# RWKV-7 decay: the low-rank product per pair in channel-major form, and the running sum by a scan

## The chip, the cores and the metric

The kernel runs on one core of a Trainium2 chip. The metric is the device time of one execution in microseconds (us), median of several runs. TensorE is PE in the profile (PEld its weight loads), VectorE is DVE, ScalarE is ACT, GpSimd is POOL and SyncE is SP. A line such as L621 is a line of the kernel before, unless it is said to be of the changed one.

## The reference

One decoder block over 512 tokens of width 2048: an input projection, RWKV-7 time mixing (16 heads of 64) beside sliding-window attention, gated merge, output projection, and a gated convolutional FFN. The change touches only the decay of the time mixing:

```python
w = -jax.nn.softplus(-(w0 + jnp.tanh(wd) @ w2)) - 0.5
decay = jnp.exp(-jnp.exp(w.astype(f32)))
...
def step(state, inp):
    r_t, k_t, v_t, w_t, ka_t, kb_t = inp
    sa = jnp.einsum('bhvk,bhk->bhv', state, ka_t)
    state = (state * w_t[:, :, None, :] + sa[..., None] * kb_t[:, :, None, :]
             + v_t[..., None] * k_t[:, :, None, :])
    y = jnp.einsum('bhvk,bhk->bhv', state, r_t)
    return state, y
```

Here wd has 96 columns and w2 is 96 x 1024. The recurrence over 512 steps is computed in chunks of 64 steps, for which the kernel needs, per channel, the product of the decays from the start of a chunk up to each step. Since exp(w) = exp(-0.5) * sigmoid(w0 + tanh(wd) @ w2), the logarithm of that product is a running sum of sigmoids times -exp(-0.5).

## The kernel before

The weights of the big projections are f32 values split into two f32r parts (whi, wlo), and so are the activations (xhi, xlo); a 128x128 block of weights takes three products (L260 to L262, output acc, 512 tokens wide). ScalarE makes whi, VectorE makes wlo. DMAs fill four raw tiles ahead of that.

After the first norm comes attention, then the RWKV stage, about 315 to 1205 us of the span. It works on eight pairs of heads (128 channels each). Each pair p goes through three functions:

- early(p) projects k, r and v, and makes the normalised keys and the decays. Here is the change. thw (tanh(wd), with a row of ones for w0) is computed once, 128 x 512 with the low rank on partitions.
- late(p) builds the chunk matrices, inverts triangular systems in five rounds of f16 products (L728 to L751), and walks the eight chunks (L755 to L772): psG (two halves of 64 rows), copy G on VectorE, psU, two copies UV (ScalarE the upper half, VectorE the lower), psS (two halves), update SV on VectorE, and from there the next psG. L779 and L781 beside them collect the output.
- final(p) normalises and gates the output.

The calls stand in the order late(p), early(p+1), final(p), and then three gate projections. The order in which each engine issues is not the order of the code: a scheduler in the tile framework builds it from dependencies and its own estimates, and it interleaves the projection products and early(p+1) with the chunk walk of late(p), so that TensorE has other work while VectorE and ScalarE pass results along the chain. Each engine then issues its list strictly in that order, waiting on semaphores.

In early(p) the decay goes like this before the change. Four products of 128 tokens (L621) take thw as the stationary operand and w2 as the moving one, so that tokens lie on partitions: ps[tokens, channels]. ScalarE applies Tanh, VectorE adds 1 (L624; with 0.5 * (tanh(x/2) + 1) this is twice the sigmoid). Four more products (L628) with the constant K["tri"], ones where two tokens are in the same chunk and in order, sum over tokens and turn the result around: ps[channels, tokens]. Two Exp (L629, L631) make Et, the decay product with a leading column of ones, and Ei, its inverse. Et and Ei are used in late(p), in BKK and BAR (L666 to L669), which feed the first products L689. bulk is a ring of three PSUM tiles, shared by nearly all products of the stage.

Of the kernel before, what the change touches and what calls it, by code (L numbers as in the profile page):

```python
# [8 lines left out]
F32 = mybir.dt.float32  # L9
# [3 lines left out]
AF = mybir.ActivationFunctionType  # L13
ALU = mybir.AluOpType
# [4 lines left out]
P = 128  # L19
S = 512  # L20
NT = S // P
HD = 64
C = 64
# [5 lines left out]
SQE = float(np.exp(-0.5))  # L29
# [5 lines left out]
class Dims:  # L35
# [37 lines left out]
CONST_PARTS = (  # L73
    ("ident", 128), ("strict", 64), ("incl", 64), ("istack", 64),
    ("m1", 64), ("m2", 64), ("m4", 64), ("m8", 64), ("m16", 64), ("m32", 64),
    ("t1bd", 128), ("idsg", 128), ("tri", 128), ("bo", 128), ("cen", 128), ("sel2", 2), ("ones", 128), ("dist", 256),
)
CONST_AT = {}
_at = 0
# [6 lines left out]
def shape_constants():  # L86
    out = np.zeros((P, NCONST), np.float32)

    def put(nm, a):
        o, n = CONST_AT[nm]  # L90
        out[:, o : o + n] = a
# [4 lines left out]
    t = np.arange(C)[None, :]  # L96
# [7 lines left out]
    si, ti = i[:, None], i[None, :]  # L104
    put("t1bd", (si == ti) | ((si // 2 == ti // 2) & (si > ti)))
    same = si // C == ti // C
    put("tri", same & (si <= ti))
    put("bo", same)
    put("cen", (si == ti) - same / float(C))
    put("sel2", si // C == np.arange(2)[None, :])  # L110
# [2 lines left out]
    dist = (BLK + si - kj).astype(np.float32)  # L113
# [21 lines left out]
def block_kernel(ctx: ExitStack, tc: tile.TileContext, d: Dims, a: dict, out: bass.AP):  # L135
    nc = tc.nc
    act, dve, pool, pe, sync = nc.scalar, nc.vector, nc.gpsimd, nc.tensor, nc.sync
# [145 lines left out]
    if True:  # L283
# [233 lines left out]
        with ExitStack() as pr:  # L517
# [21 lines left out]
            def bulk():  # L539
                return blk.tile([P, S], F32, name="bulk", tag="bulk")  # L540
# [15 lines left out]
            for i in range(NG):  # L556
                acc = ztile(d.c_gd + i * P)
                t = wtile("lw")
# [19 lines left out]
            pool.memset(SV[C:P, 0, 1], 0.0)  # L578
            Et = bd.tile([P, NCH, C + 1], F32, name="Et")
            pool.memset(Et[:, :, 0:1], 1.0)  # L580
            AI = bd.tile([P, 2, NCH, P], F16, name="AI")
            BT = bd.tile([P, 2, NCH, P], F16, name="BT")
            def r3(ap, c=C):
                return ap.rearrange("p (n c) -> p n c", c=c)
# [14 lines left out]
            def early(p):  # L599
# [16 lines left out]


                ps = bulk()
                for t in range(NT):
                    ts = slice(t * P, (t + 1) * P)  # L620
                    pe.matmul(ps[:, ts], thw[:, ts], w2, start=True, stop=True)  # L621
                lg = wtile("lw")
                act.activation(lg, ps, AF.Tanh, scale=0.5)
                dve.tensor_scalar(lg, lg, 1.0, None, op0=ALU.add)  # L624
                ps = bulk()
                for t in range(NT):
                    ts = slice(t * P, (t + 1) * P)
                    pe.matmul(ps[:, ts], lg[:, ts], K["tri"], start=True, stop=True)  # L628
                act.activation(Et[:, :, 1:], r3(ps), AF.Exp, scale=-0.5 * SQE)  # L629
                Ei = wtile("Ei")  # L630
                act.activation(Ei, ps, AF.Exp, scale=0.5 * SQE)  # L631

                ps = bulk()
                lora(ps, ag, 0, 1)
# [772 lines left out]
```

## Time and profile before

| what | value |
|---|---|
| time, median of 3 runs | 2952.3 us (2951.39 to 2952.68) |
| span of the profiled execution (first to last instruction) | 2946.4 us |
| TensorE busy | 2897.7 us, 98% |
| VectorE busy | 1949.0 us, 66% |
| ScalarE busy | 1316.0 us, 45% |
| GpSimd busy | 219.4 us, 7% |
| mean granted TensorE clock | 0.997 |
| chain that ended last, by engine | PE 92%, DVE 3%, ACT 2%, DMA 2% |

The page gives the span of the profiled execution and no other time of it; the median of the runs stands 5.9 us above that span. Busy time of TensorE is modelled from overlapping matmuls, so its share says that the queue is never empty for long, not that each product runs at its best; the distance from one start to the next tells what a product costs.

### The profile page before, as it was taken

Reading aid. Unit: us, or ns where it says so; the run is one execution under the profiler, and the core shown is the slowest. Engines: PE = TensorE matmul, PEld = TensorE weight load, DVE = VectorE, ACT = ScalarE, POOL = GpSimd, SP = SyncE. Lnnn points to the kernel's source line nnn. Section 1 sums busy time; section 2 is a strip of 40 time slices with the busy share of each in tenths; the row PEclk is TensorE's granted clock in tenths of the full one; section 3 lists DMA queues with packets and bytes.
Section 4 is the critical chain, followed back from the end, with each engine's and each line's share of the span. In section 5 each row is a group of like instructions: output and inputs, shape, how many; then the busy total and the mean of one; then the engine's idle time right before and its main releaser. Section 6 shows DMA issues by size and latency. Waiting matters only on the chain.

```text
span 2946.4 us, 48467 instructions
## 1 busy us (share of the span) xinstructions
PE 2897.7 (98%) x18922; PEld 2473.2 (84%) x18922; DVE 1949.0 (66%) x3242; ACT 1316.0 (45%) x2134; POOL 219.4 (7%) x286
## 2 busy tenths in 40 slices
PE   7999999999999999999999899999999999999999
PEld 6777777777777777688888899999999999888887
DVE  5555666666666666344567877778777778665555
ACT  4344434434334334232346554554554555544444
POOL 0001000000000000101000011011011011000000
PEclk9999999999999999999999999999999999999999
DMA  6855656656656656878877788888888888877775
GB/s 185 210 151 153 178 139 154 159 129 161 158 131 162 155 129 170 250 223 262 275 243 247 193 242 236 230 227 225 234 239 235 227 229 237 311 240 242 256 258 189
DMA packets 225142, 609.47 MB, mean 207 GB/s; under 512 B 24768, under 2 KB 44944, under 8 KB 223888
## 3 DMA queue, kind: packets, MB, share of 16 engines
q1 hardware_dynamic: 157504, 434.92, 45.9%
q0 software_dynamic: 36064, 132.14, 23.3%
q10 hardware_dynamic: 31344, 39.31, 3.9%
q8 instruction: 148, 2.42, 0.3%
q14 instruction: 82, 0.67, 0.1%
HBM read 556.62 MB, written 174.43 MB: 248 GB/s over the span
## 4 chain that ended last, share of the span: by engine, by line
PE 92%; DVE 3%; ACT 2%; DMA 2%; issue 1%; ACTq 0%; SPq 0%; DVEq 0%
PE X L1108 17%; PE X L975 11%; PE acc L262 10%; PE acc L261 10%; PE acc L260 10%; PE Y L975 8%; PE Y L1108 8%; PE Z L1108 4%; PE psG L758 1%; PE bulk L689 1%; PE mi L505 1%; PE bulk L751 1%; PE psS L769 1%; PE bulk L728 1%; DMA raw<-in_w_z_dram 1%
## 5 line engine op out<-in xcount | busy, mean ns | idle before, releaser
L262 PE MATMUL acc<-xhi,wlo 128*128 128x512 f32 x1120 | 460.0, 411 | 0.7 <-DVE wlo L244 0.7
L260 PE MATMUL acc<-xhi,whi 128*128 128x512 f32 x1120 | 454.9, 406 | 4.0 <-ACT whi L243 4.0
L261 PE MATMUL acc<-xlo,whi 128*128 128x512 f32 x1120 | 453.9, 405 | 0.0
L243 ACT ACTIVATE whi<-raw 128x512 fp32r<-128x512 f32 x352 | 220.0, 629 | 491.3 <-PE acc L261 326.2
L968 DVE TENSOR_TENSOR wlo<-raw,whi 128x1024 fp32r<-128x1024 f32 x210 | 257.0, 1224 | 203.4 <-ACT whi L967 202.4
L244 DVE TENSOR_TENSOR wlo<-raw,whi 128x512 fp32r<-128x512 f32 x352 | 240.3, 688 | 205.1 <-ACT whi L243 198.1
L967 ACT ACTIVATE whi<-raw 128x1024 fp32r<-128x1024 f32 x210 | 222.6, 1060 | 289.3 <-PE X L975 151.8
L1108 PE MATMUL X<-b,whi 128*128 128x256 f32 x1472 | 270.4, 284 | 2.3 <-DVE u L1128 0.9
L1108 PE MATMUL X<-t,whi 128*128 128x256 f32 x1408 | 258.9, 284 | 8.7 <-DVE u L1128 8.3
L1091 DVE TENSOR_TENSOR wlo<-raw,whi 128x1024 fp32r<-128x1024 f32 x176 | 215.1, 1223 | 77.5 <-ACT whi L1090 77.2
L1108 PE MATMUL Y<-t,whi 128*128 128x256 f32 x1408 | 257.1, 283 | 0.0
L262 PEld LDWEIGHTS acc<-xhi,wlo 128*128 128x128 f32 x1120 | 211.3, 189 | 44.2 <-issue 3.1
L260 PEld LDWEIGHTS acc<-xhi,whi 128*128 128x128 f32 x1120 | 211.6, 189 | 43.2 <-ACT whi L243 5.2
L261 PEld LDWEIGHTS acc<-xlo,whi 128*128 128x128 f32 x1120 | 211.3, 189 | 40.3 <-issue 3.1
L1090 ACT ACTIVATE whi<-a 128x1024 fp32r<-128x1024 f32 x132 | 139.3, 1056 | 216.4 <-DVE a L1084 213.2
L1108 PEld LDWEIGHTS X<-b,whi 128*128 128x128 f32 x1472 | 230.7, 193 | 3.1 <-issue 2.4
L1108 PEld LDWEIGHTS X<-t,whi 128*128 128x128 f32 x1408 | 220.8, 193 | 9.3 <-DVE u L1128 5.7
L1108 PEld LDWEIGHTS Y<-t,whi 128*128 128x128 f32 x1408 | 219.6, 192 | 0.0
L1108 PE MATMUL X<-b,wlo 128*128 128x256 f32 x736 | 209.1, 284 | 2.1 <-DVE wlo L1091 2.1
L1091 DVE TENSOR_TENSOR wlo<-a,whi 128x1024 fp32r<-128x1024 f32 x132 | 161.7, 1226 | 68.2 <-ACT whi L1090 67.6
L1108 PE MATMUL X<-t,wlo 128*128 128x256 f32 x704 | 200.1, 284 | 0.1
L1108 PE MATMUL Y<-t,wlo 128*128 128x256 f32 x704 | 199.2, 283 | 0.0
(346 smaller groups left out, 6151.2 us busy)
## 6 DMA issues: line engine op xcount, KB each, us to landing
raw<-in_w_up_dram SPq DMA_DIRECT2D x180, 512.0 KB
raw<-in_w_z_dram SPq DMA_DIRECT2D x288, 256.0 KB
s_dn<-in_w_dn_dram POOLq DMA_DIRECT2D x88, 512.0 KB, 6.3
raw<-in_w_up_dram POOLq DMA_DIRECT2D x88, 512.0 KB, 8.7
raw<-s_dn SPq DMA_DIRECT2D x88, 512.0 KB
raw<-in_w_dn_dram SPq DMA_DIRECT2D x66, 512.0 KB
a<-in_w_up_dram SPq DMA_DIRECT2D x48, 512.0 KB
s_dn<-in_w_dn_dram SPq DMA_DIRECT2D x44, 512.0 KB
```

Source lines behind the costliest of these rows:

```text
L243: pin(act.activation(hi, raw, AF.Copy))
L244: pin(dve.tensor_tensor(lo, raw, hi.bitcast(F32), op=ALU.subtract))
L260: pe.matmul(acc, whi[:, j], xhi[:, k], start=first, stop=False)
L261: pe.matmul(acc, whi[:, j], xlo[:, k], start=False, stop=False)
L262: pe.matmul(acc, wlo[:, j], xhi[:, k], start=False, stop=last)
L505: pe.matmul(ps[:, h], pT[:, kb, h], vt[:, n - 1 + kb, g * HD : (g + 1) * HD], start=kb == kbs[0], stop=kb == kbs[-1])
L967: act.activation(whi, wr, AF.Copy)
L968: dve.tensor_tensor(wlo, wr, whi.bitcast(F32), op=ALU.subtract)
L975: pe.matmul(dst, l[:, q, ts], r[:, es], start=fst and j == 0, stop=lst and j == 2, skip_group_check=True)
L1090: pin(act.activation(hi, t, AF.Copy))
L1091: pin(dve.tensor_tensor(lo, t, hi.bitcast(F32), op=ALU.subtract))
L1108: pin(pe.matmul(ps, l[:, k], r[:, k], start=start and k + i == 0, stop=last and i == 2, skip_group_check=True))
```

## The change

The product is formed channel-major at once: w2 is the stationary operand and thw, all 512 tokens of it, the moving one, so that one product gives ps[channels, tokens]. Tanh and the +1 are the same instructions on that layout. The running sum is then one instruction on VectorE, tensor_tensor_scan along the 512 tokens: state = going * state + lg, where the tile going holds ones, and a zero at the first token of each chunk, so that the sum starts anew there. It writes Ei; the first Exp reads Ei and writes Et, and the second turns Ei into its inverse in place. The constant "tri" leaves the table of constants (128 columns less), and GpSimd fills going once, before the pairs.

```diff
-    ("t1bd", 128), ("idsg", 128), ("tri", 128), ("bo", 128), ("cen", 128), ("sel2", 2), ("ones", 128), ("dist", 256),
+    ("t1bd", 128), ("idsg", 128), ("bo", 128), ("cen", 128), ("sel2", 2), ("ones", 128), ("dist", 256),
...
-    put("tri", same & (si <= ti))
...
+            going = bd.tile([P, S], F32, name="going")
+            pool.memset(going, 1.0)
+            pool.memset(going.rearrange("p (n c) -> p n c", c=C)[:, :, 0:1], 0.0)
...
                 ps = bulk()
-                for t in range(NT):
-                    ts = slice(t * P, (t + 1) * P)
-                    pe.matmul(ps[:, ts], thw[:, ts], w2, start=True, stop=True)
+                pe.matmul(ps, w2, thw, start=True, stop=True)
                 lg = wtile("lw")
                 act.activation(lg, ps, AF.Tanh, scale=0.5)
                 dve.tensor_scalar(lg, lg, 1.0, None, op0=ALU.add)
-                ps = bulk()
-                for t in range(NT):
-                    ts = slice(t * P, (t + 1) * P)
-                    pe.matmul(ps[:, ts], lg[:, ts], K["tri"], start=True, stop=True)
-                act.activation(Et[:, :, 1:], r3(ps), AF.Exp, scale=-0.5 * SQE)
                 Ei = wtile("Ei")
-                act.activation(Ei, ps, AF.Exp, scale=0.5 * SQE)
+                dve.tensor_tensor_scan(Ei, going, lg, 0.0, op0=ALU.mult, op1=ALU.add)
+                act.activation(Et[:, :, 1:], r3(Ei), AF.Exp, scale=-0.5 * SQE)
+                act.activation(Ei, Ei, AF.Exp, scale=0.5 * SQE)
```

The scheduler makes new lists from this, in the RWKV stage alone. On TensorE, before, in early(2) beside the chunk walk of pair 1, this stood from the first triangle product (L628: bulk<-cst,lw) to the psU that follows the product for the learning rate (L597):

```order
L628 MATMUL bulk<-cst,lw 128x128
L769 MATMUL psS<-UV,KK 64x64
L779 MATMUL bulk<-MM,UV 64x64
L781 MATMUL bulk<-BAR,SV 64x64
L628 MATMUL bulk<-cst,lw 128x128 x2
L758 MATMUL psG<-SV,AB 64x64
L628 MATMUL bulk<-cst,lw 128x128
L758 MATMUL psG<-SV,AB 64x64
L597 MATMUL bulk<-ads,wl 128x512
L762 MATMUL psU<-G,BX 128x64
```

Just ahead of that stand the four L621 (bulk<-wl,thw), cut up in the same way by a psG, and then an acc, the psU and two acc of that chunk. In the changed kernel (its own line numbers: L621 is the new product, L599 the learning rate, L755 psG, L759 psU, L766 psS, L776 and L778 the output, L259 to L261 acc) the same place reads:

```order
L621 MATMUL bulk<-thw,wl 128x512
L755 MATMUL psG<-SV,AB 64x64 x2
L599 MATMUL bulk<-ads,wl 128x512
L759 MATMUL psU<-G,BX 128x64
L260 MATMUL acc<-xlo,whi 128x512
L261 MATMUL acc<-xhi,wlo 128x512
L766 MATMUL psS<-UV,KK 64x64
L776 MATMUL bulk<-MM,UV 64x64
L778 MATMUL bulk<-BAR,SV 64x64
L259 MATMUL acc<-xhi,whi 128x512
L766 MATMUL psS<-UV,KK 64x64
```

The product for the learning rate has moved up by one chunk, both halves of psG stand together, and an acc stands between the halves of psS where a triangle product stood. Of the eight psG of a pair three now stand whole in this way, before only one.

On VectorE, at the same place (L760 or L757 copies G, L764 or L761 copies UV, L771 or L768 updates SV), before:

```order
L760 COPY G<-psG 128x64
L624 TENSOR_SCALAR lw<-lw 128x512
L764 COPY UV<-psU 64x64
L771 SCALAR_TENSOR_TENSOR SV<-SV,ee,psS 64x64 x2
L760 COPY G<-psG 128x64
```

and now, where the scan is listed as a SCALAR_TENSOR_TENSOR into Ei:

```order
L757 COPY G<-psG 128x64
L624 TENSOR_SCALAR lw<-lw 128x512
L626 SCALAR_TENSOR_TENSOR Ei<-going,lw 128x512
L761 COPY UV<-psU 64x64
L768 SCALAR_TENSOR_TENSOR SV<-SV,ee,psS 64x64 x2
```

The scan has come between the +1 and the copy of UV's lower half, and the SV update stands behind both. On ScalarE the two Exp stay close together behind the Tanh, but one UV copy that stood behind the second of them and ahead of the next projection work now stands behind that work:

```order
L760 ACTIVATE UV<-psU 64x64
L627 ACTIVATE Et<-Ei 128x8x64
L633 ACTIVATE lw<-bulk,half 128x512
L628 ACTIVATE Ei<-Ei 128x512
L532 ACTIVATE zpad_2702<-acc,par 128x512
L242 ACTIVATE whi<-raw 128x512
L760 ACTIVATE UV<-psU 64x64
```

The first Exp (L627), which reads the scan, and four more instructions now stand ahead of the UV copy of the next chunk but one.

## The prediction

> **What bounds the kernel now.** I read the first part of the page (busy time by engine), then the waits of TensorE inside the RWKV stage, then the timeline of one pair, row by row. The page says that TensorE is the bound of the whole program:
>
> ```profile
> span 2946.4 us, 48467 instructions
> ...
> PE 2897.7 (98%) x18922; PEld 2473.2 (84%) x18922; DVE 1949.0 (66%) x3242; ACT 1316.0 (45%) x2134; POOL 219.4 (7%) x286
> ```
>
> The changed lines run only in the RWKV stage, from about 315 to 1205 us. The waits of PE in 300 to 1210 us (engine, line, whom it waited for: us in total, times, longest) are all there are:
>
> ```profile
> PE bulk L728 <- ACT AI L206: 1.8, 7, 0.3
> PE bulk L689 <- DVE bon L656: 1.3, 1, 1.3
> PE bulk L381 <- DVE rq L197: 1.3, 7, 0.3
> PE acc L262 <- DVE wlo L244: 0.7, 1, 0.7
> PE bulk L728 <- ACT XIW L206: 0.3, 1, 0.3
> ```
>
> That is 5.4 us in 910 us. In this stage, too, the matmul queue is the clock: VectorE and ScalarE are late nowhere that PE would show, because projection products (acc) stand between the dependent ones. So a microsecond of PE work taken out of this stage is a microsecond of the span, unless something new is late.
>
> A long PE row in the timeline is no price, since matmuls overlap; the price of a piece is the distance from its start to the start of the next PE row. These are the rows of pair 2's decay (start us, us, engine, line, what; the last row, from a second look at the timeline, is the same place one pair later):
>
> ```profile
> 509.19 0.71 PE L621 MATMUL bulk<-wl,thw 128*128 128x128 f32 x4
> 509.83 0.33 PE L758 MATMUL psG<-SV,AB 128*64 128x64 f32 x2
> 510.09 0.49 PE L621 MATMUL bulk<-wl,thw 128*128 128x128 f32 x2
> 510.50 0.33 PE L758 MATMUL psG<-SV,AB 128*64 128x64 f32 x2
> 510.76 0.49 PE L621 MATMUL bulk<-wl,thw 128*128 128x128 f32 x2
> 511.01 0.48 PE L261 MATMUL acc<-xlo,whi 128*128 128x512 f32 x1
> ...
> 512.60 0.49 PE L628 MATMUL bulk<-cst,lw 128*128 128x128 f32 x2
> 513.01 0.33 PE L769 MATMUL psS<-UV,KK 128*64 128x64 f32 x2
> ...
> 513.50 0.71 PE L628 MATMUL bulk<-cst,lw 128*128 128x128 f32 x4
> 514.15 0.33 PE L758 MATMUL psG<-SV,AB 128*64 128x64 f32 x2
> 514.40 0.49 PE L628 MATMUL bulk<-cst,lw 128*128 128x128 f32 x2
> 514.82 0.33 PE L758 MATMUL psG<-SV,AB 128*64 128x64 f32 x2
> ...
> 515.08 1.13 PE L597 MATMUL bulk<-ads,wl 128*128 128x512 f32 x2
> ...
> 620.59 0.71 PE L621 MATMUL bulk<-wl,thw 128*128 128x128 f32 x4
> ```
>
> The pair repeats after 620.59 - 509.19 = 111.40 us. A product in f32 stands as two records, so "L621 x4" is two of the four products.
>
> **Part 1: the triangle product L628 goes.** In this pair its eight records fill the queue from 512.60 to 513.01 (0.41), 513.50 to 514.15 (0.65) and 514.40 to 514.82 (0.42): 1.48 us.
>
> **Part 2: L621, four products of 128 columns, becomes one of 512.** It holds the queue from 509.19 to 509.83 (0.64), 510.09 to 510.50 (0.41) and 510.76 to 511.01 (0.25): 1.30 us. The new product has the shape of L597 (128x512, f32, two records). The chain that ended last (start us, us, what) has that shape, and both decay products in pair 0 where nothing stands between their pieces:
>
> ```profile
> 319.50 0.89 PE bulk L621 x8
> ...
> 321.64 1.13 PE bulk L628 x8
> ...
> 405.57 0.86 PE bulk L597 x2
> 406.43 0.27 PE psG L758 x4
> ```
>
> L597 cost 0.86 there, and 0.96 where it follows a 64-wide product (515.08 to the psU at 516.04 in the timeline). I take 0.86 since the chain's share is its own streaming; 0.96 stays as the other end. Saved: 0.44 us (0.34 to 0.44). Pieces that stand alone among 64-wide products cost about half as much again as in one run: 1.30 and 1.48 against 0.89 for L621 in pair 0.
>
> Here a rule speaks against this part. The Trainium skill (TensorE: Matmul & The Clock Gate, Step-by-step: what each phase is for) has it that matmul throughput is a matter of the columns that stream, and that the next weights load under the running product. By it four times 128 columns cost as much as 512, part 2 saves nothing, and part 1 saves only what the same columns stream. The row of pair 0, 0.89 against 0.86, agrees; the interleaved rows do not. What that gives is worked out as the first rival below.
>
> **Part 3: the neighbours.** Before, each psG (L758) in this pair but one is cut in two by another product, and its halves cost 0.26 + 0.25 (509.83 to 510.09; 514.15 to 514.40). Uncut it costs 0.27 (the chain's last row). In the changed order three of the eight psG stand whole, two more than before: 2 x 0.24 = 0.48 us saved. The projection products are as many as before and only change places; I set that at nothing, with ends of +0.2 (one more acc run of the 57 in a pair, and dearer places) and -0.4 us.
>
> **Part 4: the scan on VectorE.** No row shows a scan. Below it bounds the two-input operation over the same 128x512 f32 tile, above it twice the dearest VectorE row of the stage (line, operation, shapes, count | busy us, mean ns):
>
> ```profile
> L685 DVE TENSOR_TENSOR BKE<-BKK,ee 128x1024 f32<-128x1024 f32 x8 | 9.8, 1221 | 0.1
> ...
> L652 DVE SCALAR_TENSOR_TENSOR lw<-rz,par,k 128x512 f32<-128x512 f32 x8 | 6.0, 751 | 0.2
> ```
>
> So 0.75 to 2.44 us, and I take 1.22: each of 512 outputs needs the one before it, and the nearest row for a tile at half the rate is the one of 1024 elements. The Trainium skill (DVE: opcode table, instruction layouts, handler registers and perf-mode slots, section 6, Datapath and trigger behaviour) says that the built-in scan runs at half throughput; an estimate from that page would be the same 1.22, and no run so far shows it. VectorE has room for 1.22 us more in 111.4; what counts is who queues behind it. In the changed order of VectorE the scan stands behind the +1 (L624) and ahead of the copy UV<-psU, for which the second half of psS waits. The rows of before give both sides of that race:
>
> ```profile
> 511.29 0.60 ACT L623 ACTIVATE lw<-bulk 128x512 f32<-128x512 f32 x1 [2.91 <-PE bulk L621]
> 511.32 0.33 PE L762 MATMUL psU<-G,BX 128*128 128x64 f32 x2
> 511.46 0.47 PE L262 MATMUL acc<-xhi,wlo 128*128 128x512 f32 x1
> 511.78 0.40 PE L260 MATMUL acc<-xhi,whi 128*128 128x512 f32 x1
> 511.92 0.43 DVE L624 TENSOR_SCALAR lw<-lw 128x512 f32<-128x512 f32 x1 [0.82 <-ACT lw L623]
> 512.10 0.33 PE L769 MATMUL psS<-UV,KK 128*64 128x64 f32 x2
> ...
> 512.38 0.23 DVE L764 COPY UV<-psU 64x64 f32<-64x64 f32 x1
> ...
> 517.78 0.50 PE L262 MATMUL acc<-xhi,wlo 128*128 128x512 f32 x1
> ...
> 518.21 0.33 PE L769 MATMUL psS<-UV,KK 128*64 128x64 f32 x2
> ```
>
> PE in the new order: new product 0.86, psG 0.27, L597 0.96, psU 0.14 (511.32 to 511.46), two acc at 0.32, first half of psS with its two companions 0.50 (512.10 to 512.60), one acc 0.43 (517.78 to 518.21): 3.80 us, so the second half of psS comes up 3.80 us after the new product starts. VectorE: Tanh starts 0.28 after PE has gone on from the product (511.01 to 511.29), +1 starts 0.63 after Tanh and takes 0.43, then the scan, then the copy with 0.23, and 0.12 to the matmul (511.78 + 0.20 to 512.10 is how the other half follows ScalarE's copy): 0.86 + 0.28 + 0.63 + 0.43 + scan + 0.23 + 0.12 = 2.55 + scan. The wait is then scan - 1.25 us where that is positive: nothing at 0.75 and at 1.22, 1.19 us per pair at 2.44. The slack is thin: 0.03 us.
>
> On ScalarE the Exp of Et now waits for the scan with four instructions and then a UV copy behind it. At 0.6 each (the row of L623) they are done 3.0 us after the scan, at 2.20 + 1.22 + 3.0 = 6.4 us; the psU that this copy reads comes behind the rest of psS (0.50), two psG halves (0.52) and seven acc (0.32 each), at 3.80 + 3.26 = 7.1. Covered at 1.22; at 2.44 late, but then PE is late as well. The two Exp read SBUF in place of PSUM, 128x512 both ways: I set that at nothing.
>
> **Part 5: the rest.** Two memsets on GpSimd, of which one is 128x512, half the size of this one at 268.6 us:
>
> ```profile
> L571 POOL MEMSET BV<- x1: 969/969/969, 268.6 to 268.6; 128x1024 f32 x1
> ```
>
> They are needed at pair 0's scan at about 321 us: covered by some 40 us. The constants' DMA is 128 columns smaller and lands long before the stage: nothing. The bulk PSUM ring loses one buffer per pair: nobody waits for it in the list of waits, so nothing.
>
> **Pair 0** has no chain of an earlier pair around it, and its pieces stand together: L628 1.13 and 0.03 of L621, 1.16 us at most. The scan falls into idle time of VectorE, 3.01 us that ended with this row:
>
> ```profile
> 324.50 0.55 DVE L646 TENSOR_SCALAR k<-lw,half 128x512 f32<-128x512 f32 x1 [3.01 <-ACT lw L636]
> ```
>
> Against that, PE waits there for bon (1.3 us, in the list), which hangs on VectorE, so the saved PE time may turn into wait: 0 to 1.16, taken as 1.16 because that wait stands at the end only and later work of the queue can move up.
>
> **The sum.** Pairs 1 to 7: 7 x (1.48 + 0.44 + 0.48) = 16.8; pair 0: 1.2; in all 18.0 us. The profiled span of 2946.4 becomes 2928.4; the median of the runs lies 5.9 us above that span (2952.3), and with the same 5.9 the time is 2934.3 us. 0.2% (5.9 us) is about what a measurement of this kernel tells from no change.
>
> **The rivals.**
> Only streaming counts: the pieces' extra price in the interleaved rows is wait for the neighbours' operands and stays. Then each pair saves what the columns cost, 0.89 by pair 0's row: 8 x 0.89 = 7.1 us, 2945.2. For it: pair 0's rows. Against it: in pair 2 a record pays 0.205 (512.60 to 513.01 for two) where its run costs 0.11 in pair 0, and the list of PE's waits has none for these lines.
> The chain psG, G, psU, UV, psS, SV sets the pair's length and PE's freed time becomes wait: no gain, 2952. For it: weight loads do wait inside the chain,
>
> ```profile
> PEld psS L769 <- ACT UV L763: 19.2, 54, 0.4
> ```
>
> against it: acc products are there to fill, and the whole stage shows 5.4 us of PE idle. The same row is the room for more: if acc products moved between the halves take a third of these 19.2 us away and the ends of part 3 hold, the gain is 18.0 + 6.4 + 2.8 = 27.2 us, 2925.
> Slower: the scan holds VectorE so long that the second half of psS waits for its copy by more than the 2.40 us that a pair saves. By the race above this needs a scan of over 1.25 + 2.40 = 3.65 us. At 5 us it costs 7 x 1.35 = 9.5, less pair 0's 1.2: 2960.6. No VectorE row of this tile speaks for such a price.
>
> **How the numbers follow.** The main case 0.70: 2934.3, by the ends of parts 2 to 4 from 2931.5 (acc at -0.4 per pair: 18.0 + 2.8 saved) to 2945.9 (scan 2.44, acc +0.2, 0.96 for the product, pair 0 nothing: 7 x (2.40 - 1.19 - 0.2 - 0.1) = 6.4). The larger gain 0.07, only streaming 0.11, no gain 0.08, slower 0.04. The range of 2925 to 2945.5 leaves out no gain, slower and a few hundredths at both ends. Faster by over 0.2% (below 2946.4): main, larger gain and most of streaming, 0.85; within 0.2%: 0.11; slower 0.04.
>
> **What would show it.** Right: no rows for the triangle; one product of two records at about 0.43 each; pairs repeating after some 109 us in place of 111.4; a scan row near 1.22 us with the UV copy right behind it; PE waits in the stage still near 5 us. Wrong: a new PE wait for UV or SV each pair (scan too long, or ScalarE's UV late behind the Exp); the period unchanged with acc rows stretched; pair 0 as long as before while the others shrink (its VectorE work is then the bound). What happens behind 1215 us should only shift: the orders of all engines are the same there.

## The result and the profile after

The changed kernel takes 2932.2 us (median of 4 runs, 2930.29 to 2935.18); the kernel before, run beside it, 2952.5 us (4 runs, 2951.39 to 2956.64). The ratio is 0.9926, with a 95% interval of 0.9913 to 0.9938: about 20 us less. The profiled execution of the changed kernel took 2935.18 us by its own time, with a span of 2933.4 us, so 1.8 us lie around the span. First the page:

```profile
span 2933.4 us, 48233 instructions
...
PE 2879.3 (98%) x18810; PEld 2453.2 (84%) x18810; DVE 1959.2 (67%) x3250; ACT 1319.0 (45%) x2134; POOL 219.4 (7%) x288
```

PE lost 112 records: 64 of the triangle and 48 of the narrow products (64 became 16). It is as full as before, 98%. VectorE grew by 10.2 us, of which the eight scans are 9.8. Next, the waits of PE in 300 to 1210 us (line, whom it waited for: us in total, times, longest):

```profile
PE bulk L686 <- DVE bon L653: 1.9, 1, 1.9
PE bulk L725 <- ACT AI L205: 1.8, 7, 0.3
PE acc L261 <- DVE wlo L243: 1.7, 2, 1.4
PE bulk L380 <- DVE rq L196: 0.7, 2, 0.6
PE psU L759 <- DVE G L757: 0.3, 1, 0.3
```

That is 6.4 us against 5.4 before, and no row has a wait for UV or SV once per pair: nothing new is late in every pair. The place of the change in pair 2, by the timeline (start us, us, engine, line, what):

```profile
508.65 1.12 PE L621 MATMUL bulk<-thw,wl 128*128 128x512 f32 x2
509.70 0.34 PE L755 MATMUL psG<-SV,AB 128*64 128x64 f32 x4
509.81 0.60 ACT L623 ACTIVATE lw<-bulk 128x512 f32<-128x512 f32 x1 [1.97 <-PE bulk L621]
509.97 1.12 PE L599 MATMUL bulk<-ads,wl 128*128 128x512 f32 x2
510.11 0.22 DVE L757 COPY G<-psG 128x64 f32<-128x64 f32 x1 [0.97 <-PE psG L755]
510.44 0.43 DVE L624 TENSOR_SCALAR lw<-lw 128x512 f32<-128x512 f32 x1
510.90 1.23 DVE L626 TENSOR_TENSOR_SCAN Ei<-going,lw 128x512 f32<-128x512 f32 x1
510.93 0.33 PE L759 MATMUL psU<-G,BX 128*128 128x64 f32 x2
...
512.16 0.23 DVE L761 COPY UV<-psU 64x64 f32<-64x64 f32 x1
512.16 0.64 ACT L627 ACTIVATE Et<-Ei 128x512 f32<-128x512 f32 x1 [0.64 <-DVE Ei L626]
512.21 0.50 PE L259 MATMUL acc<-xhi,whi 128*128 128x512 f32 x1
...
512.63 0.33 PE L766 MATMUL psS<-UV,KK 128*64 128x64 f32 x2
```

The product holds the queue from 508.65 to 509.70, 1.05 us; psG stands whole behind it for 0.27 (509.70 to 509.97); the scan runs 1.23 us with the UV copy right behind it. The same product comes one pair later at

```profile
618.25 1.12 PE L621 MATMUL bulk<-thw,wl 128*128 128x512 f32 x2
```

so this pair lasts 109.60 us, and the later ones 108.96 to 109.14, against 111.40 before.

### The profile page after: what moved, and what is told of

It is laid out like the page before. It is cut to its first block, busy times and chain, and to the rows that moved or that the text cites. A ratio compares the mean times of both kernels' runs of the same rounds, so it can differ in the third digit from the quotient of the medians.

```text
span 2933.4 us, 48233 instructions
## 1 busy us (share of the span) xinstructions
PE 2879.3 (98%) x18810; PEld 2453.2 (84%) x18810; DVE 1959.2 (67%) x3250; ACT 1319.0 (45%) x2134; POOL 219.4 (7%) x288
## 4 chain that ended last, share of the span: by engine, by line
PE 91%; DVE 3%; DMA 3%; ACT 2%; issue 1%; ACTq 0%; SPq 0%; DVEq 0%; POOLq 0%
PE X L1105 16%; PE X L972 11%; PE acc L261 11%; PE acc L260 10%; PE acc L259 10%; PE Y L972 8%; PE Y L1105 8%; PE Z L1105 4%; PE bulk L686 1%; DMA raw<-in_w_up_dram 1%; PE mi L504 1%; PE bulk L748 1%; PE psG L755 1%; PE psS L766 1%; PE bulk L725 1%
## 5 line engine op out<-in xcount | busy, mean ns | idle before, releaser
L259 PE MATMUL acc<-xhi,whi 128*128 128x512 f32 x1120 | 456.1, 407 | 5.2 <-ACT whi L242 5.2
L261 PE MATMUL acc<-xhi,wlo 128*128 128x512 f32 x1120 | 459.4, 410 | 1.7 <-DVE wlo L243 1.7
L965 DVE TENSOR_TENSOR wlo<-raw,whi 128x1024 fp32r<-128x1024 f32 x210 | 257.1, 1225 | 203.6 <-ACT whi L964 201.9
L259 PEld LDWEIGHTS acc<-xhi,whi 128*128 128x128 f32 x1120 | 211.3, 189 | 44.8 <-ACT whi L242 6.4
L261 PEld LDWEIGHTS acc<-xhi,wlo 128*128 128x128 f32 x1120 | 211.0, 188 | 44.9 <-DVE wlo L243 4.4
L1088 DVE TENSOR_TENSOR wlo<-a,whi 128x1024 fp32r<-128x1024 f32 x132 | 161.7, 1225 | 67.4 <-ACT whi L1087 66.7
```

The source lines that it names most:

```text
L259: pe.matmul(acc, whi[:, j], xhi[:, k], start=first, stop=False)
L261: pe.matmul(acc, wlo[:, j], xhi[:, k], start=False, stop=last)
L965: dve.tensor_tensor(wlo, wr, whi.bitcast(F32), op=ALU.subtract)
L1088: pin(dve.tensor_tensor(lo, t, hi.bitcast(F32), op=ALU.subtract))
```

## The experiments

Three numbers are given for each kernel. The time is a median, with its ratio to the kernel before of the same batch. The period is the mean distance from one pair's first decay product to the next over three late pairs. The stage runs from pair 0's first decay product to a fixed product behind the last pair (the one 11,000 records from the end of PE's list, at about 1200 us), so it leaves out what wanders elsewhere in the span. e1 to e4 ran together on one chip, then a_changed_again, e6, e8 and b_before_again on a second, e9 and e10 on a third, e11 and c_changed_third on a fourth.

| kernel | time us (range) | ratio, 95% interval | period us | stage us |
|---|---|---|---|---|
| before, first profile | 2952.5 (2951.39 to 2956.64) | | 111.40 | 897.4 |
| b_before_again | 2953.1 (one run) | | 111.33 | 899.0 |
| changed, first profile | 2932.2 (2930.29 to 2935.18) | 0.9926 [0.9913, 0.9938] | 109.02 | 882.0 |
| a_changed_again | 2935.7 (2934.11 to 2937.85) | 0.9936 [0.9923, 0.9950] | 109.00 | 881.3 |
| c_changed_third | 2934.9 (2932.32 to 2935.99) | 0.9933 [0.9920, 0.9947] | 109.03 | 880.0 |
| e1_four_narrow | 2942.1 (2939.8 to 2947.16) | 0.9957 [0.9942, 0.9971] | 110.30 | 891.2 |
| e2_scan_twice | 2938.0 (2934.6 to 2939.71) | 0.9939 [0.9926, 0.9953] | 108.89 | 882.4 |
| e3_no_scan | 2936.6 (2935.05 to 2937.79) | 0.9936 [0.9922, 0.9950] | 108.92 | 881.5 |
| e4_no_triangle | 2932.2 (2928.6 to 2934.71) | 0.9921 [0.9907, 0.9934] | 108.54 | 880.2 |
| e6_kk_later | 2933.9 (2930.66 to 2935.46) | 0.9929 [0.9916, 0.9941] | 109.1 | 880.7 |
| e8_scan_four | 2938.0 (2935.43 to 2939.47) | 0.9943 [0.9931, 0.9956] | 109.17 | 883.6 |
| e9_four_no_scan | 2932.1 (2929.11 to 2932.51) | 0.9925 [0.9913, 0.9938] | 108.49 | 878.4 |
| e10_long_scan | 2930.6 (2926.51 to 2932.34) | 0.9925 [0.9912, 0.9939] | 107.43 | 876.2 |
| e11_scan_768 | 2932.5 (2928.8 to 2936.22) | 0.9925 [0.9912, 0.9938] | 108.12 | 878.7 |

The kernel before took a median of 2954.5, 2955.3, 2953.9 and 2954.8 us in the four batches.

The second table says where a late pair's PE queue goes, in us per pair, by the distance from each record's start to the next record's start:

| kernel | triangle | L621 | psG | acc | psS | MM,UV and BAR,SV | period |
|---|---|---|---|---|---|---|---|
| b_before_again | 1.48 | 1.30 | 4.21 | 74.67 | 2.02 | 4.52 | 111.33 |
| a_changed_again | 0 | 1.06 | 3.70 | 74.85 | 1.92 | 4.25 | 109.00 |
| e1_four_narrow | 0 | 1.39 | 4.21 | 75.56 | 1.92 | 4.30 | 110.30 |
| e4_no_triangle | 0 | 1.38 | 3.71 | 74.25 | 1.90 | 4.27 | 108.54 |
| e9_four_no_scan | 0 | 1.39 | 3.69 | 74.23 | 1.91 | 4.25 | 108.49 |
| e10_long_scan | 0 | 1.06 | 3.70 | 74.45 | 1.70 | 3.42 | 107.43 |
| e11_scan_768 | 0 | 1.06 | 3.20 | 74.29 | 1.69 | 4.77 | 108.12 |

What is left out (the products of the inversion, BKE, BX and the rest, some 23 us) agrees within 0.3 us in all of them.

### e1_four_narrow: the wide product cut into four, the scan kept

```diff
-                pe.matmul(ps, w2, thw, start=True, stop=True)
+                for t in range(NT):
+                    ts = slice(t * P, (t + 1) * P)
+                    pe.matmul(ps[:, ts], w2, thw[:, ts], start=True, stop=True)
```

> The changed kernel, but its product channel-major in four pieces of 128 tokens again (w2 loaded four times), with the scan kept. Theory (what counts is TensorE's queue, and a narrow piece that stands alone among 64-wide products costs twice its streaming): part 2 of the prediction is given back, 0.44 us per pair, and one psG is cut again, 0.24: 7 x 0.68 = 4.8 us above the changed kernel, 2935 to 2938 us, pairs repeating after 109.6 to 109.9 us. Rival (only streamed columns count): the same time as the changed kernel, within 1.5 us of 2932, and the period unchanged at 109.1.

Four pieces give back 9 to 11 us of the 18 in the stage, about twice the 4.8 us that I expected (1.6 of them is the half clock of pair 0, told of below); the rival, no change at all, fell. By the table a late pair of e1 is 1.30 us longer than one of a_changed_again, but the last of the three contains a single wait of 0.72 us for wlo; in the other two the difference is 1.01 us: the pieces 0.33, psG cut again 0.51, acc 0.40, the other groups -0.23. The dearer acc hold a wait that the changed kernel does not have in each pair. It stands in the list of PE's waits, and in the timeline at the second half of psS:

```profile
PE psS L768 <- DVE UV L763: 1.2, 6, 0.2
```

```profile
510.82 0.71 PE L623 MATMUL bulk<-thw,wl 128*128 128x128 f32 x4
...
512.72 1.02 PE L599 MATMUL bulk<-ads,wl 128*128 128x512 f32 x2
512.92 0.60 ACT L625 ACTIVATE lw<-bulk 128x512 f32<-128x512 f32 x1 [2.91 <-PE bulk L623]
...
515.55 0.33 PE L768 MATMUL psS<-UV,KK 128*64 128x64 f32 x2 [0.20 <-DVE UV L763]
```

By the prediction's race, with its 0.86 + 0.28 up to the start of Tanh replaced by what the cut product takes here (510.82 to 512.92: 2.10), the copy is ready at 2.10 + 0.63 + 0.43 + 1.225 + 0.23 + 0.12 = 4.74 us; PE starts at 515.55 - 510.82 = 4.73. So the wait is the race that the prediction worked out. But it is 0.2 us of the 1.01; the pieces themselves and the psG that they cut make up most of the loss.

### e2_scan_twice and e8_scan_four: more scans

```diff
                 dve.tensor_tensor_scan(Ei, going, lg, 0.0, op0=ALU.mult, op1=ALU.add)
+                dve.tensor_tensor_scan(Ei, going, lg, 0.0, op0=ALU.mult, op1=ALU.add)
```

(three added lines in e8_scan_four; each repeats the first and gives the same result.)

> The changed kernel with the same scan issued twice in a row into Ei: one more VectorE instruction of 1.22 us per pair and nothing else. In its order the second scan stands between the copy UV and the SV update. Theory (the scan is hidden with next to no slack): the SV update, which PE's next psG waits for, comes some 0.6 us later, of which a part is covered: 2 to 5 us above the changed kernel, 2934 to 2937 us. Rival A (VectorE has room, a scan is free): within 1.5 us of 2932. Rival B (VectorE is on the path in every pair): 8 x 1.22 = 9.8 us more, 2942 us.

> The changed kernel with the same scan issued four times: 3.7 us more of VectorE per pair, and the decay's result later by as much. The scheduler puts other VectorE work between the four. Theory after the run with two scans (VectorE has room and the order makes it usable): within 3 us of the changed kernel, period under 109.6. Rival (it only just held at two): 2.4 us more per pair for the two that are too many, 17 us above the changed kernel, period 111.4.

With a second scan the stage is 0.4 to 2.4 us longer than in the three profiles of the changed kernel (880.0 to 882.0; here 882.4), and the period is not longer (108.89 against 109.0). The rival of a VectorE on the path in every pair, 9.8 us, fell; so did the mechanism of my theory, an SV update that comes late in each pair. The median lies above the 2934 to 2937 us that I gave, but no changed kernel ran in that batch; whether a second scan costs 1 us or 4 is not settled. Four scans lengthen the stage by 2.3 us over a_changed_again and the median by 2.3, with overlapping intervals, as the theory for e8 allowed, where 24 more scans of 1.225 us are 29 us of VectorE work. The timeline of e8_scan_four shows where they went. It is VectorE beside the same chunk:

```profile
512.43 1.23 DVE L626 TENSOR_TENSOR_SCAN Ei<-going,lw 128x512 f32<-128x512 f32 x1
513.68 0.23 DVE L764 COPY UV<-psU 64x64 f32<-64x64 f32 x1
513.94 1.23 DVE L627 TENSOR_TENSOR_SCAN Ei<-going,lw 128x512 f32<-128x512 f32 x1
515.20 0.59 DVE L771 SCALAR_TENSOR_TENSOR SV<-SV,ee,psS 64x64 f32<-64x64 f32 x2
515.82 1.22 DVE L628 TENSOR_TENSOR_SCAN Ei<-going,lw 128x512 f32<-128x512 f32 x1
517.08 0.23 DVE L760 COPY G<-psG 128x64 f32<-128x64 f32 x1
517.22 1.22 DVE L629 TENSOR_TENSOR_SCAN Ei<-going,lw 128x512 f32<-128x512 f32 x1
```

The scheduler put a step of the chunk walk behind each scan, so in this order no step stands behind more than one, and VectorE has the room. What one longer scan ahead of a step does is what e10_long_scan, below, tries.

### e3_no_scan, e9_four_no_scan and e4_no_triangle: without the running sum

e3_no_scan takes the scan out of the changed kernel, e9_four_no_scan takes it out of e1_four_narrow, and e4_no_triangle takes the triangle out of the kernel before, with its four token-major products kept.

```diff
-                dve.tensor_tensor_scan(Ei, going, lg, 0.0, op0=ALU.mult, op1=ALU.add)
-                act.activation(Et[:, :, 1:], r3(Ei), AF.Exp, scale=-0.5 * SQE)
-                act.activation(Ei, Ei, AF.Exp, scale=0.5 * SQE)
+                act.activation(Et[:, :, 1:], r3(lg), AF.Exp, scale=-0.5 * SQE)
+                act.activation(Ei, lg, AF.Exp, scale=0.5 * SQE)
```

> The changed kernel without the scan: both Exp read the decay's summands in place of their running sum, so the output is not the reference's. Theory (scan hidden): 2930 to 2932 us, at most 2 us below the changed kernel, period 109.0 to 109.1. Rival (the scan stands on the path): 8 x 1.22 = 9.8 us below, 2922 us, period 107.9.

> The kernel before without the triangle products: the four token-major products stay, both Exp read their result, no scan; the running sum is left out and the output is not the reference's. Part 1 alone. Theory: 7 x (1.48 + 0.24 for a psG that stands whole) + 1.1 in pair 0, some 13 us below the kernel before: 2938 to 2941 us, period 109.6 to 109.9. Rival (only streamed columns count): 8 x 0.89 = 7 us below, 2945 us, period 110.5. The distance to the run without the scan is then part 2: 3 to 5 us by the theory, nothing by the rival.

> The changed kernel with the channel-major product cut into four of 128 tokens each, as in e1_four_narrow, and with the running sum left out as well, so the chunk's sums are not the reference's. Theory (e1's loss of some 9 us in the stage is the race of the second half of psS with the copy UV, which the scan delays and a later channel-major product leaves no room for): without the scan the race is gone; the pair's period is 108.5 to 108.9 us, as in e4_no_triangle, the stage 880 to 882 us, and the time that of e3_no_scan and e4_no_triangle, a ratio of 0.992 to 0.9935. Rival (the four pieces with the weights and the tokens in exchanged places cost by themselves, or by the order that the scheduler makes of them): period near 110 us, stage 889 to 891, a ratio near 0.9955.

e3: the stage is 881.5 us, between the profiles of the changed kernel, and the period 108.92 in place of 109.0. The scan costs nothing that can be seen; if it lay on the path, eight of them would have taken 9.8 us out. The median, 2936.6, is above the 2930 to 2932 that I expected; beside the kernel before of its own batch the ratio, 0.9936, is that of a_changed_again.

e4 has the whole gain, with no wide product at all: stage 18.8 us below b_before_again, where I expected some 13 and the rival of streamed columns 7. I had also expected that e3, with the wide product, would be 3 to 5 us faster than e4; in the same batch it was 4.4 us slower, with ranges that do not overlap, and its late pair 0.38 us longer. e4's pair is 2.79 us shorter than that of b_before_again: the triangle 1.48, psG 0.50, acc 0.42, MM,UV and BAR,SV 0.25, psS 0.12, small things the rest. The acc gain is one of neighbours. I sorted the 288 acc of a pair by what stands beside them:

| place of an acc | us each | b_before_again | a_changed_again | e4 and e9 |
|---|---|---|---|---|
| within a run | 0.229 | 185 | 184 | 181 |
| first of a run | 0.327 | 47 | 47 | 51 |
| last of a run | 0.27 to 0.28 | 47 | 47 | 51 |
| alone between narrow products | 0.41 to 0.43 | 9 | 10 | 5 |

e9 has the four narrow pieces and a period of 108.49, as e4. So the pieces cost 0.33 us more than the wide product, and their order gives 0.6 us back in acc: the wide product's own saving does not show in the time. It also means that e1's loss belongs to the pieces and the scan together: the later scan brings the wait, and with the scan in the list the scheduler cuts psG again (4.21 against 3.69). Period and ratio of e9 came as the theory had them, the stage a little below; but the reason that I had put first, the race alone, covers only the 0.2 us of wait. That the wide product is worth something in another order is not excluded; here no time shows it.

### a_changed_again, b_before_again and e6_kk_later: pair 0 and the repeat

> The changed kernel once more, as the yardstick on this chip and for a second profiled execution. Both theories: ratio to the kernel before 0.992 to 0.994; pairs repeating after 109.0 us; pair 0 at 81.5 to 82 us if its loss is a matter of the order of VectorE's list, some 79 if it was one execution's bad luck with a transfer.

> The kernel before once more, for a second profiled execution. If pair 0's 79.4 us is a matter of its order, it comes again, with the same period of 111.4; if it was luck with the transfer, pair 0 takes 80 to 82 us.

e6_kk_later moves the product of the keys with their inverse norm down to where its result is used:

```diff
-                dve.tensor_tensor(kk, kk, rb, op=ALU.mult)
...
+                dve.tensor_tensor(kk, kk, rb, op=ALU.mult)
                 kb = kz
```

> The changed kernel with one line moved: the multiplication of the keys by their inverse norms (kk by rsb, which waits for a round trip through memory) is written just ahead of its first use, so that in pair 0 a wlo and rz stand ahead of it in VectorE's list. Theory (pair 0 is longer than before because that wait holds the wlo behind it, and PE waits 1.4 us for it): PE's wait for wlo in pair 0 goes, pair 0 is 1 to 1.5 us shorter than in the changed kernel, the rest the same; 1 to 2 us below the changed kernel. Rival (pair 0 is bound by the sum of VectorE's work up to the first L689): the wait for bon grows by as much, pair 0 and the time unchanged.

Between these two repeats the stage falls by 17.7 us; over the three profiles of the changed kernel against b_before_again it falls by 17.0, 17.7 and 19.0 (against the first profile of before, whose pair 0 was short, by 15.4 to 17.4). Pair 0 differs between executions of one and the same kernel, and the traces show two things that move it. The first is a row of VectorE. In the first profile of before, in b_before_again and in a_changed_again the timeline has

```profile
329.11 0.69 DVE L615 TENSOR_TENSOR kk<-kk,rsb 128x512 f32<-128x512 f32 x1 [2.39 <-DMA rsb<-rsd]
```

```profile
331.73 0.69 DVE L615 TENSOR_TENSOR kk<-kk,rsb 128x512 f32<-128x512 f32 x1 [4.39 <-DMA rsb<-rsd]
```

```profile
331.66 0.69 DVE L617 TENSOR_TENSOR kk<-kk,rsb 128x512 f32<-128x512 f32 x1 [3.63 <-DMA rsb<-rsd]
```

VectorE waits there for a small DMA that brings the inverse norms back (rsb). It was issued at 325.5, 325.3 and 325.3 us, and the product that reads it started 3.6, 6.5 and 6.3 us later (6.3 and 6.1 in the other two profiles of the changed kernel): the first profile of before had a quick one, and its pair 0 lasted 79.43 us in place of 81.43. So the kernel before takes some 81.4 us with a slow transfer, as I expected for that case.

The second is TensorE's granted clock. In the changed kernel the transfer was equally slow three times, and yet pair 0 lasted 81.82, 80.31 and 80.58 us; for the second of these, a_changed_again, I had given 81.5 to 82 or some 79. The same eight products stand behind the wait for bon in the first profile and in a_changed_again:

```profile
344.20 3.49 PE L686 MATMUL bulk<-BAR,BKK 128*128 128x256 f32 x8 [1.88 <-DVE bon L653]
347.13 0.97 PE L261 MATMUL acc<-xhi,wlo 128*128 128x512 f32 x1
```

```profile
343.89 1.99 PE L686 MATMUL bulk<-BAR,BKK 128*128 128x256 f32 x8 [1.86 <-DVE bon L653]
345.54 0.59 PE L261 MATMUL acc<-xhi,wlo 128*128 128x512 f32 x1
```

They hold the queue for 2.93 us in the one and for 1.65 in the other. The granted clock is 0.50 from 344.54 to 347.95 us in the first, and 1.00 over the same rows in the second. From the end of that wait to the end of pair 0 the three profiles take 57.68, 56.21 and 56.20 us, so the stretch at half clock is the 1.5 us by which the first is longer here. Seven of the fourteen profiles have such a stretch in pair 0 (the first of the changed kernel, e1, e3, e6, e9, e10 and e11); what sets it off is not shown, since equally long waits stand without one in the others.

The same DMA also cost a_changed_again 1.43 us in pair 1. There its reader started 8.1 us after the issue, and in VectorE's list the copy of UV stands behind that reader:

```profile
410.17 0.69 DVE L617 TENSOR_TENSOR kk<-kk,rsb 128x512 f32<-128x512 f32 x1 [2.12 <-DMA rsb<-rsd]
```

```profile
411.17 0.33 PE L766 MATMUL psS<-UV,KK 128*64 128x64 f32 x2 [1.43 <-DVE UV L761]
```

Without the half clock in the one and this wait in the other, the stage of the changed kernel would be about 880 us in all three profiles (880.5, 879.9 and 880.0).

In e6 the wait of PE for wlo in pair 0 is gone, and PE is through its wait for bon 23.1 us after the pair's start, against 24.1 to 24.4 in the changed kernel: that is 1.0 to 1.3 us earlier, about the 1 to 1.5 that the theory expected. The wait for bon did not grow by as much, as the rival had it; it is 2.1 us against 1.9:

```profile
PE bulk L686 <- DVE bon L653: 2.1, 1, 2.1
```

But the clock was halved behind that wait here too, and the pair lasts 80.78 us. e6's median is 1.8 us below a_changed_again with overlapping ranges; that it is faster was not shown.

### e10_long_scan, e11_scan_768 and c_changed_third: one longer scan

```diff
-            going = bd.tile([P, S], F32, name="going")
-            pool.memset(going, 1.0)
+            going2 = bd.tile([P, 2 * S], F32, name="going")
+            lg2 = bd.tile([P, 2 * S], F32, name="lg2")
+            pool.memset(lg2, 0.0)
+            pool.memset(going2, 1.0)
+            going = going2[:, S:]
...
-                dve.tensor_scalar(lg, lg, 1.0, None, op0=ALU.add)
-                Ei = wtile("Ei")
-                dve.tensor_tensor_scan(Ei, going, lg, 0.0, op0=ALU.mult, op1=ALU.add)
+                dve.tensor_scalar(lg2[:, S:], lg, 1.0, None, op0=ALU.add)
+                dve.tensor_tensor_scan(lg2, going2, lg2, 0.0, op0=ALU.mult, op1=ALU.add)
+                Ei = lg2[:, S:]
```

(e11_scan_768 has 768 columns in place of 2 * S and 256 in place of S as the start.)

> The changed kernel with its scan drawn out to 1024 columns, the first half of them zeros, so that the result is the same; the scan should take 2.3 to 2.45 us, the upper price that the prediction allowed for it. Theory (VectorE has room at this place, because the scheduler puts more of the accumulating products ahead of the second half of psS when the scan is longer): the period stays under 109.6 us and the time within 3 us of a_changed_again. Rival (the race of the prediction: the wait is the scan's time less 1.25 us): TensorE waits 1.05 to 1.2 us per pair at psS for UV, the period is near 110.1 us, the stage 7 to 9 us longer, and the time near 2943 us, a ratio of 0.996.

> As e10_long_scan, but the scan is 768 columns wide (256 zeros ahead), so that it should take 1.70 to 1.80 us, half a microsecond less than there; the result is the same. Theory (what e10_long_scan gained is the order that the scheduler makes of TensorE's work when it believes the scan to be longer, since the queue is the clock, and its 0.3 us of wait for UV per pair was the real length of the scan): in this order a pair has 54 runs of acc in place of the changed kernel's 57, 5 acc products that stand alone in place of 10, and 5 psG in place of 3 that are whole. By 0.1 us for a run, 0.1 for one that stands alone and 0.24 for a psG that is whole that is 0.3 + 0.5 + 0.5 = 1.3 us less, and with the cheaper order of the SV products seen in e10_long_scan the period is 106.5 to 107.4 us, without a wait for UV, the stage 869 to 876 us, and the time 5 to 12 us below that of c_changed_third. Rival (order and neighbours give nothing that lasts, e10_long_scan was a lucky run): period 109 us, the same time as c_changed_third within 3 us.

> The changed kernel once more, as the measure for e11_scan_768 on the same chip: a time of 2932 to 2936 us, a ratio of 0.9925 to 0.994, a period of 109 us.

The groups by line (busy us, mean ns) of e10 and e11 give the scan's price at the two lengths:

```profile
L628 DVE TENSOR_TENSOR_SCAN lg<-going,lg 128x1024 f32<-128x1024 f32 x8 | 18.3, 2291 | 0.3
```

```profile
L628 DVE TENSOR_TENSOR_SCAN lg<-going,lg 128x768 f32<-128x768 f32 x8 | 14.1, 1758 | 0.3
```

The wait that the race predicts is there in both, in the lists of PE's waits of e10 and e11, at 0.33 and 0.35 us in six of the pairs:

```profile
PE psS L769 <- DVE UV L764: 2.0, 6, 0.3
```

```profile
PE psS L769 <- DVE UV L764: 2.1, 6, 0.4
```

and in the timeline of e10 one sees both sides of it:

```profile
511.01 1.12 PE L624 MATMUL bulk<-thw,wl 128*128 128x512 f32 x2
...
513.27 2.29 DVE L628 TENSOR_TENSOR_SCAN lg<-going,lg 128x1024 f32<-128x1024 f32 x1
...
515.59 0.23 DVE L764 COPY UV<-psU 64x64 f32<-64x64 f32 x1
...
515.87 0.33 PE L769 MATMUL psS<-UV,KK 128*64 128x64 f32 x2 [0.34 <-DVE UV L764]
```

PE starts the second half of psS 515.87 - 511.01 = 4.86 us after the product; 2.55 + 2.29 = 4.84 by the prediction's formula. In e11 it is 4.33 against 2.55 + 1.758 = 4.31. The rival for e10, a wait of over 1.05 us and a longer pair, fell: the wait is 0.33 us, because the scheduler put four acc, not two, between psU and the first half of psS. The theory's bound on the period held, and the time is 5.2 us below a_changed_again's, on another chip, where 3 were given; the pair is 1.6 us shorter, which neither had said, since MM,UV and BAR,SV cost 0.83 us less, psS 0.22 and acc 0.40 (with the wait in it). In e11 psG is 0.50 cheaper as counted and acc 0.56, but the wait stays (PE's second psS comes earlier in that order) and BAR,SV is not cheaper: 0.9 us per pair in place of the 1.6 to 2.5 expected, and 1 to 3 us of the stage. The theory for e11 missed its period, its stage and its time. c_changed_third came as expected.

Is either better than the changed kernel? e11's median is 2.4 us below c_changed_third's on the same chip, e10's lower than all three medians of the changed kernel, but not run beside it; the intervals of the ratios overlap throughout. The stages of both contain the half clock of pair 0 (1.5 us). Two profiles with shorter pairs speak for it, the times do not settle it, and what a scheduler makes of a scan that is twice as long as needed is no method.

## Why the prediction was right

2934.3 us was forecast, 2932.2 measured, within the range; the sign was the one given 0.85. By its steps:

- **What bounds the stage.** Right. PE's queue gave back what was taken from it, and its waits in the stage are 6.4 us in place of 5.4.
- **Part 1, the triangle, 1.48 us.** Right to the hundredth: b_before_again has 1.48 us of it in a late pair, and e4_no_triangle, which takes it away alone, loses that and, with the neighbours, 2.79 us a pair.
- **Part 2, the product, 0.44 us (0.34 to 0.44).** Mis-sized. The new product holds the queue for 1.05 to 1.06 us, not 0.86, nor the 0.96 that I kept as the other end; L621 saved 0.24 us. The step that failed is "I take 0.86 since the chain's share is its own streaming": a share of the chain is not a distance between starts. In the timeline of the kernel before that same L597 takes 406.36 - 405.41 = 0.95:

```profile
405.08 0.49 PE L628 MATMUL bulk<-cst,lw 128*128 128x128 f32 x2
405.41 1.02 PE L597 MATMUL bulk<-ads,wl 128*128 128x512 f32 x2
406.36 0.34 PE L758 MATMUL psG<-SV,AB 128*64 128x64 f32 x4
```

  Record by record the trace shows where the rest comes from. An f32 record of 512 columns costs 0.43 us among products with 128 columns of weights (128*128 in the rows); right behind one with 64 columns of weights (128*64: psG, BAR,SV) it costs 0.53, right ahead of one 0.52. The L597 above pays ahead of psG, 0.95; L599 of the changed kernel, between psG and a psU of 128*128, pays behind psG, 0.96 (509.97 to 510.93). The new product, between BAR,SV and psG, pays on both sides: 0.86 + 0.10 + 0.09 = 1.05, and its two records take 0.53 and 0.52, not the 0.43 that the prediction gave as a sign of being right. Both extra prices stood in the timeline before. The product's value for the kernel is nothing that could be shown: e9 without the wide product is no slower than e3 with it.
- **Only streaming counts, the first rival.** Fell: its sum was 2945.2, and the measured time lies 13 us below; e4, where it gave 2945, took 2932.2. Pieces pay at their edges as the wide product does: a record of 128 columns costs 0.11 us inside a run and about 0.21 right behind or right ahead of a product with 64 columns of weights. The triangle's three groups are 8 x 0.11 + 6 x 0.10 = 1.48, so the extra went with the pieces; it was no wait that stayed. Behind this rival stood the rule of the Trainium skill (TensorE: Matmul & The Clock Gate, Step-by-step: what each phase is for); the rows agree with it only within a run (0.89 against 0.86). For part 2 by itself the rival's outcome, nothing saved, is what the times show, but not for its reason: the four pieces hold the queue for 1.39 us in e9 and the wide product for 1.06, and the dearer neighbours of the wide product make up the difference.
- **Part 3, the neighbours, 0.48 us.** psG fell from 4.21 to 3.70, by 0.51. The acc term, set at nothing, came at +0.18 (74.67 to 74.85), at the edge of its bound of +0.2: one more stands alone. MM,UV, BAR,SV and psS, which I had not costed, gave 0.37.
- **Part 4, the scan.** 1.225 us against 1.22. From the two lengths, (2291 - 1225) / 512 = 2.08 ns per column, and 1225 - 512 x 2.08 = 160 ns beside it; 768 columns by this are 1757 ns, and 1758 were measured. The page of the changed kernel has an ordinary two-input row at the same two widths:

```profile
L965 DVE TENSOR_TENSOR wlo<-raw,whi 128x1024 fp32r<-128x1024 f32 x210 | 257.1, 1225 | 203.6 <-ACT whi L964 201.9
...
L243 DVE TENSOR_TENSOR wlo<-raw,whi 128x512 fp32r<-128x512 f32 x352 | 239.8, 688 | 198.9 <-ACT whi L242 191.2
```

  That is (1225 - 688) / 512 = 1.05 ns per column: the scan goes at half that rate. The Trainium skill (DVE: opcode table, instruction layouts, handler registers and perf-mode slots, section 6, Datapath and trigger behaviour) says half throughput for the built-in scan; these rows agree.
- **The race.** The copy's side, 2.55 us plus the scan, held to 0.02 us in e10 and e11. In the changed kernel the copy starts at 512.16, and a psS that waits starts 0.28 after it (515.59 to 515.87 in e10): 512.44, which is 3.79 after the product's start, against 3.775 worked out. PE's side was 3.98 and not 3.80, 0.19 of that from the dearer product, which did not make Tanh later: it starts 1.16 us after the product's start (508.65 to 509.81), worked out as 0.86 + 0.28 = 1.14. So the mistake of part 2 widened the slack from 0.03 to 0.19 us, and that is luck. What failed, and only the longer scans showed it, is the bound at 2.44 us: it held the order fixed, and the order changes with the scan.
- **Part 5.** No wait in the stage is for the memsets, the constants or bulk. Right.
- **Pair 0, 1.16 us.** Not confirmed. a_changed_again and b_before_again give 80.31 against 81.43, which is 1.12, but the first profiles give 81.82 against 79.43, the sign that the prediction had named as wrong. The slow transfer and the half clock, each in some executions only, move pair 0 by 2.0 and 1.5 us, more than the term. Where the transfer was slow, PE is through the wait for bon 24.1 to 24.4 us after the pair's start in the changed kernel and 25.2 in b_before_again: 0.8 to 1.1 us less.
- **The sum.** A late pair shrank by 2.33 us against 2.40, the stage by 17.0 to 19.0 us against 18.0. Part 2 was 0.2 us too good and acc 0.18 dearer than nothing, and the chain's other products, which had no term, made that up with 0.37: that the sum agrees so closely is luck.
- **From span to time.** The last step, 5.9 us, was wrong in kind. Every profiled execution whose own time is known lies 1.8 us above its span (2935.18 and 2933.4; 2953.12 and 2951.3 in b_before_again). The first profile of before, 2946.4, was thus a quick execution of some 2948.2 us, and the 5.9 joined it to the median of others. Its span is 4.9 us shorter than that of b_before_again: 0.6 us ahead of the stage, 1.6 in it (the quick DMA in pair 0 alone 2.0), 2.7 behind. It did the forecast no harm, since in the end the 18.0 us are taken from the median. The medians fell by about 20 us where the stage fell by about 18; the intervals of the ratios (0.9913 to 0.9938 in the first comparison, 18 to 26 us) do not separate the two. The profiles show no gain outside: behind the stage lie 1730 and 1732 us in the kernel before and 1731 to 1733 in the changed one. Where the 2 us come from stays open.
- **The rivals.** Only streaming counts: fell, above. The chain sets the pair: fell, since PE's waits for the chain did not grow. The slower case needed a scan of over 3.65 us by its sum, and the scan takes 1.225; at 2.29 us e10 was not slower than the changed kernel. The larger gain did not come. Its mechanism, less waiting of weight loads in the chain, did not come either, not even in e10, whose pair is shorter: the 19.2 us of the prediction's row are 20.2 in the changed kernel and 20.5 in e10.

## What to carry to other kernels

Where one queue is the clock, price a piece by the distance to the next start at its own place, and price again each neighbour that it cuts in two: here the removed product gave 1.48 us a pair and its neighbours 0.6 to 1.3 more, while making four products into one gave nothing that the time showed. For a longer instruction on another engine, work out the race step by step (it was right to 0.02 us), but remember that a scheduler that knows the length moves both sides of it. Before a span is turned into a time, ask for the profiled execution's own time; before a spread of a microsecond or two is explained, look at the granted clock.

## What the runs showed of the hardware

- The f32r product acc, 128x512, costs 0.229 us in a run, 0.327 as the first behind narrow products, 0.27 to 0.28 as the last, and 0.41 to 0.43 alone between narrow ones. The same instruction varies by a factor of 1.8 with no wait in the list.
- An f32 record that stands next to a product with 64 columns of weights (psG, BAR,SV) costs about 0.10 us more on each such side: 0.43 becomes 0.53 or 0.52 at 512 columns, 0.11 becomes 0.21 at 128. A psU, with 128 columns of weights, behind it costs nothing more.
- A scan of 128 rows takes 1225, 1758 and 2291 ns for 512, 768 and 1024 columns.
- The DMA that brings rsb back let its reader start 3.6 us after issue in one execution of the kernel before and 6.5 in another; pair 0 lasted 79.43 and 81.43 us in them.
- The granted clock fell to 0.50 for 3.4 us in pair 0 of seven profiles of fourteen, the same kernel with and without it; eight products then took 2.93 us in place of 1.65.
